# Reading position biases as one run of 157 numbers and spreading them on VectorE, in a hybrid attention and state-space kernel on Trainium2

## The chip, the cores and the metric

The kernel runs on one core of one Trainium2 chip. The metric is device time in microseconds of one execution; less is better. The time before is the median of three runs, 1765.67 us (1764.33 to 1768.28).

A core has five engines that each work through a queue of their own, in order: TensorE (matmuls, in the profile PE, its weight loads PEld), VectorE (DVE), ScalarE (ACT), GpSimd (POOL) and SyncE (SP, which in this kernel only issues DMAs). Data sits in SBUF, 128 partitions wide, and matmul results in PSUM, eight banks of 128 x 512 numbers here. Engines wait for each other through semaphores.

## The reference, cut to what matters

Two layers over 256 latent tokens of width 2048 and 256 context tokens. The first layer has 16 heads of 2-D neighbourhood attention beside a bidirectional state-space mixer; the second is a gated short convolution. The change touches the attention's position bias:

```python
GRID_W, NA_HEADS, NA_KH, NA_KW = 64, 16, 8, 16
rows = seq // GRID_W                       # 4 rows of 64 columns
kh = min(NA_KH, rows)                      # 4: every key row is seen
...
dc_idx = jnp.clip(col[None, :] - col[:, None], -(NA_KW - 1), NA_KW - 1) + NA_KW - 1
...
dr_idx = rs + jnp.arange(kh) - r + NA_KH - 1
bias = rpb[:, dr_idx[None, :, None], dc_idx[:, None, :]].reshape(nh, GRID_W, kh * GRID_W)
s_lat = jnp.einsum('bqhd,bkhd->bhqk', qr, kb).astype(jnp.float32) * scale + bias.astype(jnp.float32)
s_lat = jnp.where(mask, s_lat, -jnp.inf)
```

`rpb` has, for each head, 15 row differences x 31 column differences. A query at row r and column q needs, for key row a and key column b, the number at row difference a - r + 7 and column difference b - q + 15. Outside a window of 16 columns the score is masked, so what is added there does not matter as long as it is finite. Scores against the 256 context tokens have no bias. A softmax runs over 256 latent and 256 context keys.

## The kernel before, in words

**Weights.** All large matmuls take float32 inputs in two parts, a high part (a rounded copy, type fp32r) and a low part (the rest), and three products make one: high x high, high x low, low x high. Weights come from HBM in pieces of 128 x 1024 numbers (512 KB) into buffers called `raw` (`issue`, line 428, on SP's queue). ScalarE makes the high part `wH` (`split`, line 458), VectorE the low part `wL` (`low_part`, line 465), and the `raw` buffer is free again; TensorE multiplies (`mm`, line 231). There are three pairs of `wH` and `wL`. The same queue brings the pieces of the modulation matrix `in_ada_w`, which VectorE folds into a running sum (line 857).

**Order.** Nothing is scheduled at run time. While the program is built, a planner (`Plan`) keeps a clock for each engine and one for the DMA queue and prices every instruction. Side work is written as generators that yield what they wait for: `W_("DVE", bt)` goes on when the planner's clock of VectorE has room and `bt` is planned to be ready within 400 ns (`may`, lines 296 to 318). Between groups of matmuls, `pump` lets every such task go on as far as it can. A DMA on SP is priced in `Plan.add` with 450 ns of SP's time, and its bytes at 270 B per ns on the planner's DMA clock:

```python
            self.t[e] = s + (1200 if e == "POOL" else 450)
            if e == "SP":
                self.dma = max(self.dma, s + 1000) + n / self.RATE
```

A VectorE instruction with two full inputs is priced by the number of its elements. So the order of the instructions on each queue follows from these prices.

**Stages.** The modulated inputs are made (to about 200 us), then come the input projections, group by group (four heads of attention, two groups of the state-space mixer), with the attention heads and the state-space groups as side work between the matmuls; the last attention heads end near 1200 us. Then the output projection, the second layer's projections and its output follow.

**The bias.** Before the first head, one DMA (line 967) copies, for each head, 320 of the 15 x 31 numbers of `rpb`, from the 76th on, to an HBM scratch `rpbs` of [16, 64, 320], 64 times over: one copy for each query column. A bias buffer (two of them, `bias0` and `bias1`, taken in turn by the heads) is `bt`, 128 x 3 x 256: three blocks of 256 numbers in each partition. Block 0 is the bias of the first 128 queries (grid rows 0 and 1), block 1 of the other 128 (rows 2 and 3), each for 4 key rows x 64 key columns; partition p is grid row p // 64 of its half and query column p % 64. Block 2 is zero and stands for the context keys.

Each head (`head_gen`) first issues, on SP, four loads, one for each query row r, to 64 partitions of block r // 2 (line 1080). A partition gets four pieces of 64 numbers, 31 apart in the scratch, since neighbouring key rows are 31 numbers apart in `rpb`. The step of 319 between partitions in a scratch with rows of 320 slides the window by one number for each query column. VectorE then adds the mask in place, in one instruction over 2 x 4 x 64 numbers (line 1085). Later `top` (line 1098) adds the bias to the scores of a half, taking the row maximum at once. Loads of the head after the next must wait until this head's result is out (line 1077).

The steps that the prediction speaks of besides: `dt_gen` loads a row of biases and decay rates (`in_rows`, line 1184) to 128 partitions with SP's queue, and VectorE uses it at line 1203; this happens near the first two heads' bias loads. Shifted reads in the convolution of the second layer are at line 1856, a read of the same kind without a shift at line 1411.

Of the kernel before, what the change touches and what calls it, by code (L numbers as in the profile page):

```python
# [11 lines left out]
ALU = mybir.AluOpType  # L12
# [159 lines left out]
def kernel(ctx: ExitStack, tc, x, cx, ada_w, ada_b, w_in, w_out, sc_in, sc_out, rpb, small, const,  # L172
# [9 lines left out]
    V, S, G, T, DMA = nc.vector, nc.scalar, nc.gpsimd, nc.tensor, nc.sync  # L182
    DMA2 = nc.scalar
    plan = Plan()
    E = plan.add
# [214 lines left out]
    ident, strip, mask, mhalf = C_("ident"), C_("strip"), C_("mask"), C_("mhalf")  # L400
# [673 lines left out]
    def head_gen(a, h):  # L1074
        hd = 4 * a + h
        bt, s4 = bias[hd % 2], s4s[hd % 4]
        yield when(lambda: hd < 2 or ("pv", hd - 2) in got)
        yield W_("SP")
        for r in range(4):
            E(DMA.dma_start(bt[64 * (r % 2):64 * (r % 2) + 64, r // 2, :].rearrange("p (a b) -> p a b", a=4),  # L1080
                            bass.AP(tensor=b0.tensor, offset=b0.offset + hd * 64 * 320 + (7 - r) * 31 - 61,
                                    ap=[[319, 64], [31, 4], [1, 64]])))
        yield W_("DVE", bt)
        bv = bt[:, 0:2, :].rearrange("p q (r c) -> p (q r) c", c=64)
        E(V.tensor_tensor(out=bv, in0=bv, in1=mask.unsqueeze(1).to_broadcast([128, 8, 64]), op=ALU.add))
        sps = {}

        def score(qt):
# [461 lines left out]
    for h in range(4):  # L1550
        spawn(side, head_gen(0, h))
# [11 lines left out]
    def do_qk(a, nxt):  # L1563
        psQ = banks(2)
        proj(512, "act", psQ, 4)
        spawn(urgent, kq_gen("Q", a, psQ, 2, statq, QT, True), 2)
        psK = banks(4)
        proj(512, "act", psK, nxt)
        spawn(urgent, kq_gen("K", a, psK, 4, statk, KT, True), 4)
        for h in range(4):  # L1570
            spawn(side, head_gen(a, h))
# [432 lines left out]
```

## Time and profile before

The profiled execution took 1762.67 us; from its first to its last instruction it is 1760.9 us. The runs shown for comparison have their median 3.0 us above it.

| what | value |
|---|---|
| median of 3 runs | 1765.67 us |
| profiled execution | 1762.67 us, span 1760.9 us |
| mean granted TensorE clock | 0.999 |
| bias loads (line 1080) | 64 of 64 KB |
| mask adds (line 1085) | 16, mean 682 ns, 10.7 us together |
| DMA packets under 512 B | 34,304 of 147,629 |
| DMA engines' share by SP's queue | 64.0% |

How to read it. Busy time is time in which an engine executes; the profile also tells after which event an engine that stood idle went on ("releaser"). The chain that ended last is followed back from the last instruction, at each step to what released it. A DMA's issue is an instruction on the queue of its engine (SPq, POOLq); its data lands later. "x64" is a count; three durations with slashes are the least, the median and the greatest in ns. In the rows by stretch of time, each engine has its busy time and in brackets its instructions; then come TensorE's granted clock, the mean busy share of the 16 DMA engines (it can come out slightly over 1 in short stretches, since a packet counts where it begins) and what they moved in GB/s. In rows in order of time the first number is the start, the second the time until the last of the merged instructions ended, both in us; a bracket at the end is idle time of that engine before it and its releaser.

### The profile page before, as it was taken

What the parts mean: (1) busy time and instruction counts of PE and PEld (TensorE: products, weight loads), DVE (VectorE), ACT (ScalarE), POOL (GpSimd) and SP (SyncE); (2) the same over time, 40 slices, a digit from 0 to 9 for tenths busy, and PEclk for the clock granted to TensorE, in tenths of its full rate; (3) what the DMA queues carried; (4) which work ended last, traced back from release to release, by engine and by line L of the source; (5) the groups of instructions that cost most, each with busy time, mean ns of one, the idle gap of its engine ahead of it and who ended that gap; (6) DMA issues with size and microseconds to landing.
All of it is one profiled execution on the core that took longest, in us unless ns stands there. A gap on an engine that the chain in (4) does not pass through costs nothing.

```text
span 1760.9 us, 25272 instructions
## 1 busy us (share of the span) xinstructions
PE 1728.3 (98%) x9305; PEld 1442.4 (82%) x9305; DVE 1292.8 (73%) x2041; ACT 785.3 (45%) x1186; POOL 191.0 (11%) x300
## 2 busy tenths in 40 slices
PE   6999999999999999999999999999999999999998
PEld 4677988889888889888888898888878888888887
DVE  5566877888787987786888698876667776766555
ACT  5422335454354453353453444654435444444442
POOL 0000111013111012111012101110000000000000
PEclk9999999999999999999999999999999999999999
DMA  9987675577876677866577767787766888876774
GB/s 349 344 291 252 214 227 181 181 214 241 261 227 201 190 219 248 262 193 204 170 239 227 215 188 226 224 261 253 268 216 232 265 281 266 267 248 216 219 231 158
DMA packets 147629, 412.50 MB, mean 234 GB/s; under 512 B 34304, under 2 KB 48272, under 8 KB 147504
## 3 DMA queue, kind: packets, MB, share of 16 engines
q1 hardware_dynamic: 132112, 366.64, 64.0%
q0 software_dynamic: 15392, 44.24, 8.0%
q8 instruction: 73, 1.20, 0.3%
q14 instruction: 52, 0.43, 0.1%
HBM read 386.53 MB, written 25.59 MB: 234 GB/s over the span
## 4 chain that ended last, share of the span: by engine, by line
PE 94%; DVE 2%; DMA 1%; ACT 1%; issue 1%; SPq 0%; POOL 0%; DVEq 0%; ACTq 0%; POOLq 0%
PE bank L231 93%; PE bank L235 1%; DVE wL L465 1%; DMA raw<-in_ada_w 0%; ACT wH L458 0%; DMA half<-in_rows 0%; DVE hL L804 0%; SPq L618 0%; DMA raw<-in_sc_in 0%; DVE tmp L1283 0%; DVE h L1729 0%; DVE tmp L800 0%; ACT h L1748 0%; ACT hH L798 0%; DVE xm L664 0%
## 5 line engine op out<-in xcount | busy, mean ns | idle before, releaser
L458 ACT CAST wH<-raw 128x1024 fp32r<-128x1024 f32 (+1 forms) x440 | 459.5, 1045 | 664.0 <-PE bank L231 559.6
L465 DVE TENSOR_TENSOR wL<-raw,wH 128x1024 fp32r<-128x1024 f32 (+1 forms) x440 | 532.2, 1213 | 257.4 <-ACT wH L458 255.0
L231 PE MATMUL bank<-hH,wH 128*128 128x256 f32 (+1 forms) x1040 | 341.0, 328 | 0.9 <-ACT wH L458 0.9
L231 PE MATMUL bank<-hL,wH 128*128 128x256 f32 (+1 forms) x1040 | 337.0, 324 | 0.0
L231 PE MATMUL bank<-hH,wL 128*128 128x256 f32 (+1 forms) x1024 | 331.4, 324 | 3.1 <-DVE wL L465 3.1
L231 PE MATMUL bank<-wH,h 128*128 128x512 f32 x1024 | 316.8, 390 | 1.7 <-DVE h L1729 1.7
L231 PE MATMUL bank<-wH,hH 128*128 128x512 f32 x640 | 256.0, 400 | 4.8 <-ACT hH L798 2.6
L231 PE MATMUL bank<-wL,hH 128*128 128x512 f32 x640 | 249.9, 391 | 0.3 <-DVE wL L465 0.3
L231 PE MATMUL bank<-wH,hL 128*128 128x512 f32 x640 | 249.3, 390 | 0.1
L231 PEld LDWEIGHTS bank<-wH,h 128*128 128x128 f32 x1024 | 191.9, 188 | 43.5 <-DVE h L1729 3.0
L231 PEld LDWEIGHTS bank<-hH,wH 128*128 128x128 f32 x1040 | 197.8, 190 | 18.9 <-issue 2.0
L231 PEld LDWEIGHTS bank<-hL,wH 128*128 128x128 f32 x1040 | 197.8, 190 | 15.8
L231 PEld LDWEIGHTS bank<-hH,wL 128*128 128x128 f32 x1024 | 194.6, 190 | 19.4 <-DVE wL L465 4.1
L857 DVE SCALAR_TENSOR_TENSOR acc<-raw,csil,acc 128x512 f32<-128x512 f32 x240 | 179.1, 746 | 30.9 <-DMA raw<-in_ada_w 27.2
L231 PE MATMUL bank<-wL,h 128*128 128x512 f32 x512 | 199.4, 389 | 0.2 <-DVE wL L465 0.2
L231 PE MATMUL bank<-wH,mix 128*128 128x512 f32 x512 | 160.9, 391 | 0.0
L231 PEld LDWEIGHTS bank<-wH,hH 128*128 128x128 f32 x640 | 120.1, 188 | 36.3 <-issue 7.2
L231 PEld LDWEIGHTS bank<-wH,hL 128*128 128x128 f32 x640 | 120.1, 188 | 25.4 <-DVE hL L804 0.6
L231 PEld LDWEIGHTS bank<-wL,hH 128*128 128x128 f32 x640 | 120.1, 188 | 25.0 <-DVE wL L465 1.1
L231 PEld LDWEIGHTS bank<-wL,h 128*128 128x128 f32 x512 | 96.1, 188 | 20.6 <-DVE wL L465 0.6
L231 PEld LDWEIGHTS bank<-wH,mix 128*128 128x128 f32 x512 | 96.1, 188 | 20.4 <-issue 0.5
L231 PE MATMUL bank<-wL,mix 128*128 128x512 f32 x256 | 99.7, 390 | 0.0
(276 smaller groups left out, 1856.5 us busy)
## 6 DMA issues: line engine op xcount, KB each, us to landing
raw<-in_w_in SPq DMA_DIRECT2D x209, 512.0 KB
raw<-in_ada_w SPq DMA_DIRECT2D x163, 512.0 KB
raw<-in_sc_in SPq DMA_DIRECT2D x128, 512.0 KB
raw<-in_w_out SPq DMA_DIRECT2D x64, 512.0 KB
raw<-in_sc_out SPq DMA_DIRECT2D x32, 512.0 KB
dram_ptd<-tmp POOLq DMA_DIRECT2D x32, 256.0 KB, 4.9
D<-dram_ptd POOLq DMA_DIRECT2D x64, 128.0 KB, 5.6
tmp<-dram_csr SPq DMA_DIRECT2D x32, 256.0 KB
```

The lines of the kernel that those rows point to most:

```text
L231: E(T.matmul(o, l, r, start=start, stop=stop, skip_group_check=True))
L235: E(T.transpose(o, i, ident if k == 128 else ident[:k, :k]))
L458: E(S.copy(H, v))
L465: E(V.tensor_tensor(out=Lo, in0=v, in1=H.bitcast(F32), op=ALU.subtract))
L857: E(V.scalar_tensor_tensor(out=acc, in0=v[:, j], scalar=csil[:, 2 * k + j:2 * k + j + 1], in1=acc, op0=ALU.mult, op1=ALU.add))
```

## The change

The four loads of a head no longer bring four pieces of 64 numbers to each partition but one run of 157, which holds them all: 3 x 31 + 64 = 157. The run goes to the last 157 of the block's 256 places, from place 99 on. The add of the mask then reads its first input with an access pattern of its own, four runs of 64 that begin 31 apart and so overlap, and writes the 4 x 64 places of the block as before. Input and output share the buffer: for key row a and column b it reads place 99 + 31a + b and writes place 64a + b. The number of loads, their order, the waits and the instruction count are as they were in the text of the program; the planner's price of a load changes with its bytes.

```diff
         for r in range(4):
-            E(DMA.dma_start(bt[64 * (r % 2):64 * (r % 2) + 64, r // 2, :].rearrange("p (a b) -> p a b", a=4),
+            E(DMA.dma_start(bt[64 * (r % 2):64 * (r % 2) + 64, r // 2, 99:],
                             bass.AP(tensor=b0.tensor, offset=b0.offset + hd * 64 * 320 + (7 - r) * 31 - 61,
-                                    ap=[[319, 64], [31, 4], [1, 64]])))
+                                    ap=[[319, 64], [1, 157]])))
         yield W_("DVE", bt)
-        bv = bt[:, 0:2, :].rearrange("p q (r c) -> p (q r) c", c=64)
-        E(V.tensor_tensor(out=bv, in0=bv, in1=mask.unsqueeze(1).to_broadcast([128, 8, 64]), op=ALU.add))
+        run = bt[:, 0:2, 99:]
+        E(V.tensor_tensor(out=bt[:, 0:2, :].rearrange("p q (r c) -> p q r c", c=64),
+                          in0=bass.AP(tensor=run.tensor, offset=run.offset, ap=[list(run.ap[0]), [256, 2], [31, 4], [1, 64]]),
+                          in1=mask.unsqueeze(1).unsqueeze(1).to_broadcast([128, 2, 4, 64]), op=ALU.add))
```

## The prediction

> **What bounds the kernel now.** I read the engine shares, the chain that ended last, and then the bias tile. The page says:
>
> ```profile
> span 1760.9 us, 25272 instructions
> PE 1728.3 (98%) x9305; PEld 1442.4 (82%) x9305; DVE 1292.8 (73%) x2041; ACT 785.3 (45%) x1186; POOL 191.0 (11%) x300
> DMA packets 147629, 412.50 MB, mean 234 GB/s; under 512 B 34304, under 2 KB 48272, under 8 KB 147504
> PE 94%; DVE 2%; DMA 1%; ACT 1%; issue 1%; SPq 0%; POOL 0%; DVEq 0%; ACTq 0%; POOLq 0%
> ```
>
> TensorE is busy for 98% of the span and carries 94% of the chain. DMA packets and VectorE work count only where they make TensorE wait. So the first question is where the touched instructions lie (instructions of the bias tile), and how long TensorE stands still in that stretch (the busy times of the stretch, then TensorE's waits in it):
>
> ```profile
> L1080 SPq DMA_DIRECT2D bias<-dram_rpbs x64: 574/615/2323, 225.1 to 1137.8; - x64
> L1085 DVE TENSOR_TENSOR bias<-bias,const x16: 650/684/704, 234.7 to 1143.1; 128x512 f32<-128x512 f32 x16
>   DMA bias<-dram_rpbs: 0.8, 1
> 225.00:1160.00 935.00, 931.54 (x5257) 798.40 (x5256) 747.16 (x1281) 432.56 (x719) 139.91 (x212) 1.00 0.69 216
> PE bank L231 <- DVE wL L465: 2.8, 2, 2.3
> PE bank L231 <- ACT Vt L1050: 0.6, 1, 0.6
> ```
>
> The 64 loads and 16 adds lie between 225 and 1160 us. The add waited for its load once in 16, for 0.8 us. In these 935 us TensorE's busy time leaves 935.00 - 931.54 = 3.46 us of idleness, of which one stop is 2.3 us. Nothing that the change does to this stretch can gain more than those 3.46 us. I take 0.2% of the time, 3.5 us, as what a measurement of this kernel can tell from no change, so the whole idle time of the stretch is just at that bound.
>
> **Where that stop comes from.** The chain of waits from 234 us, then the first column of times on VectorE and TensorE, shows it whole:
>
> ```profile
> 234.79 0.33 SPq L428
> 235.17 7.13 DMA half<-in_rows
> 242.40 0.09 DVE half L1203
> 242.74 1.23 DVE wL L465
> ...
> 234.69 1.28 DVE L1085 TENSOR_TENSOR bias<-bias,const 128x512 f32<-128x512 f32 x2
> 242.40 0.43 DVE L1203 TENSOR_TENSOR half<-half,half 128x256 f32<-128x256 f32 x1 [6.09 <-DMA half<-in_rows]
> 242.74 2.35 DVE L465 TENSOR_TENSOR wL<-raw,wH 128x1024 fp32r<-128x1024 f32 x2
> ...
> 244.01 0.39 PE L231 MATMUL bank<-hH,wL 128*128 128x256 f32 x1 [2.33 <-DVE wL L465]
> ```
>
> A small load (the row of dt biases, issued at L1184) takes 7.13 us to land. VectorE, which works in order, stands 6.09 us in front of L1203; the two low parts of the weights (L465) are behind it, and TensorE waits 2.33 us for the first. What stands ahead of that load on SP's queue is the first two heads' bias loads and five weight loads (the queue in order of time):
>
> ```profile
> 225.08 7.26 SPq L1080 DMA_DIRECT2D bias<-dram_rpbs  x8
> 232.44 1.02 SPq L428 DMA_DIRECT2D raw<-in_w_in  x2
> 233.55 0.86 SPq L428 DMA_DIRECT2D raw<-in_ada_w  x2
> 234.79 0.33 SPq L428 DMA_DIRECT2D raw<-in_w_in  x1
> SPq L1080 <- DMA raw<-in_w_in: 2.1, 1, 2.1
> ```
>
> So this is the one place where the changed loads touch TensorE: eight of the 64.
>
> **Part 1: fewer and larger packets.** From the code, a bias load goes from 64 x 4 runs of 256 B (65,536 B) to 64 runs of 628 B (40,192 B). The kernel sheds 64 x 192 = 12,288 packets, and of its 34,304 under 512 B it loses 64 x 256 = 16,384. No view times one packet, so I bound their price by single microseconds (last two columns: share of the 16 DMA engines, GB/s) and the packets of 229 to 234 us:
>
> ```profile
> 231.00:232.00 1.00, 1.00 (x7) 0.81 (x6) 0.96 (x2) 0.00 (x0) 0.00 (x0) 1.00 1.36 205
> 232.00:233.00 1.00, 1.00 (x9) 0.96 (x8) 0.83 (x2) 0.54 (x1) 0.00 (x0) 1.00 0.42 66
> 233.00:234.00 1.00, 1.00 (x10) 1.00 (x10) 0.46 (x1) 0.99 (x2) 0.00 (x0) 1.00 0.47 94
> 237.00:238.00 1.00, 1.00 (x11) 1.00 (x10) 0.00 (x0) 0.79 (x1) 0.00 (x0) 1.00 1.03 422
> DMA packets 2287, 0.90 MB, mean 180 GB/s; under 512 B 2195, under 2 KB 2195, under 8 KB 2287
> ```
>
> Weights alone (237 to 238) move 422 / 1.03 = 410 GB/s per full share; with bias packets (231 to 232) it is 205 / 1.36 = 151 GB/s. Eight bias loads are 524,288 B: 1.3 us at 410, 3.5 us at 151. Afterwards they are 321,536 B: 0.8 us at 410, 2.1 us at 151. The saving lies between 1.3 - 0.8 = 0.5 us (small packets cost nothing extra) and 3.5 - 0.8 = 2.7 us. I take the middle, 1.6 us; it is near 3.5 - 2.1 = 1.4 us as well.
>
> There is also a hole. From 232 to 234 us the DMA engines are busy 0.42 and 0.47, so (1 - 0.42) + (1 - 0.47) = 1.1 us pass unused, because SP issues the first weight load at 232.44 only, after a bias load that had waited 2.1 us. The view names an earlier weight load as what ended that wait; in the code the bias tile depends on no weight, so it may be room in the queue, which 64 packets instead of 256 would ease. This is worth between 0 and 1.1 us; I take 0.3, the low side, as the cause is only guessed.
>
> A 628-B packet against the 256-B ones is not in the trace; if each cost as much as its bytes, the above holds, and if runs were cut in two there would still be 128 for 256.
>
> The sum: the small load lands 1.6 + 0.3 = 1.9 us earlier (bounds 0.5 and 3.8), and L1203, the low part behind it and TensorE with them. TensorE can gain no more than its 2.33 us there. What is next late: the high part that the second low part needs, and TensorE's own queue:
>
> ```profile
> 238.49 1.05 ACT L458 CAST wH<-raw 128x1024 fp32r<-128x1024 f32 x1 [0.22 <-PE bank L231]
> 241.41 0.28 PE L231 MATMUL bank<-hL,wH 128*128 128x256 f32 x1
> ```
>
> That cast ended at 239.5 and TensorE has work until 241.7, so neither is late within 1.9 us: with L1203 at 240.5 the first low part ends at about 242.1 and TensorE goes on then in place of 244.01. Thus **1.9 us**, between 0.5 and 2.33.
>
> [...] This case's drop from 410 to 151 GB/s with small packets speaks against bytes alone.
>
> **Part 2: the other 56 loads.** The same saving falls on heads 2 to 15. There TensorE's idleness is 3.46 - 2.33 = 1.13 us in all, and the add waited once, for 0.8 us. What hides them: the next head's scores wait for the turn of the heads, so a bias is loaded well ahead of its use, and TensorE has projections queued. Worth nothing. SP's issue time may fall (compare a weight load's, below), but SP's queue mostly waits for buffers:
>
> ```profile
> L428 SPq DMA_DIRECT2D raw<-in_sc_in x128: 327/328/332, 1295.7 to 1648.9; - x128
> SPq L428 <- DVE wL L465: 882.3, 373, 9.2
> ```
>
> **Part 3: the add.** It has as many elements as before and stays one instruction; only its first input is read as four overlapping runs of 64 that start 31 apart, two of them at an odd word. Nearest rows, two-source instructions in SBUF, straight and shifted by one word:
>
> ```profile
> L1411 DVE SCALAR_TENSOR_TENSOR yi<-tmp,small,tmp 128x256 f32<-128x256 f32 x16 | 7.7, 484 | 0.5
> L1856 DVE SCALAR_TENSOR_TENSOR v<-u,scwh,v 128x255 f32<-128x255 f32 x16 | 7.7, 478 | 0.0
> ```
>
> 484 ns straight and 478 shifted: a start at an odd word costs nothing, and neither row suggests a gain. I take 684 ns again. The upper bound is the step between those instructions and a second pass of 255 elements, 478 ns more for each add, 16 x 0.48 = 7.6 us over a stretch in which VectorE has 935 - 747 = 188 us free. At the one critical place two adds stand ahead of L1203, at 234.69; the 6.09 us of waiting after them swallow 2 x 0.48 = 0.96 us. Zero on the path. If the shorter load took that cover away, 4 us of it would still be there.
>
> [...]
>
> **Part 4: the order.** The program's order comes from a planner that charges a load its bytes at 270 B/ns and 450 ns of SP time. A bias load's charge falls from 243 to 149 ns, under the 450 of its issue, so its planned DMA clock moves by at most 0.38 us a head. Tasks are let in with a margin of 400 ns after groups of matmuls, so some adds, and some casts behind them, can come out a group earlier or later. TensorE does the same work. Zero, with the risk priced below.
>
> **The sum.** The profiled execution took 1762.67 us, 1.8 above its span and 3.0 below the median of the runs shown, 1765.67. Less 1.9 that is 1760.8 for such an execution, and 1763.8 for the median: 0.11%, too little to tell from no change.
>
> **Rivals.**
> - *Hidden anyway.* The small load's landing is set by the five weight loads alone: 5 x 524,288 B at 410 GB/s are 6.4 us of the 7.13. [...] For it: the DMA engines are idle at 0.42 just before. Against: that hole itself comes from SP being behind the bias loads.
> - *A worse order, slower.* A bias add, or another reader of a load, comes out one place earlier on VectorE, ahead of a low part, and waits there for its packets; TensorE starves. The price is in the trace: 6.09 us of such waiting became 2.33 us on TensorE. One event cancels the gain. It decides from the third event if the gain stays (3 x 2.33 - 1.9 = 5.1 us, 1770.8) or the second if it doesn't (4.7 us, 1770.3). For it: the margin of 400 ns is close to the shift of 0.38 us, and 16 heads try. Against: plan and chip both move the landing earlier, so the add should find its data.
> - *A better order.* The other 1.13 us go too: 1765.67 - 3.46 = 1762.2, and with luck among the stops after 1160 us a little less.
> - *It does not do what it says.* The add writes where it reads. It reads word 99 + 31a + b when it writes 64a + b, 99 - 33a >= 0 words ahead, so one rising pass reads each word before it is lost. I see no case here that costs time.
>
> **How the numbers follow.** Forecast (1.4 to 2.4 us gained) 0.45; hidden 0.30; worse order beyond the bound 0.12; better order beyond it 0.07; smaller shifts of order, 1761 to 1769, the rest. The range takes in the better order with a median as far off as the runs shown lie apart, 1764.33 to 1768.28, and the second event: 1760 to 1770. Faster 0.08 and slower 0.13 are the two cases beyond the bound with a hundredth each for what the small shifts may add; same is what is left, 0.79.
>
> **What would show it.** Right: packets near 135,300, with 17,920 under 512 B; the bias adds at 0.68 us; L1203's wait under 5 us and TensorE's stop near 242 us under 1 us; TensorE's idleness in 225 to 1160 us between 1 and 3 us. Wrong: the stop unchanged (hidden); adds over 0.75 us (reading); new rows of TensorE waiting for a low part, or VectorE waiting for bias (order).

## The result and the profile after

The changed kernel takes 1781.74 us (median of 6 runs, 1777.93 to 1786.39) beside 1766.63 us for the kernel before (6 runs): a ratio of 1.0079, 95% interval 1.0063 to 1.0094; the medians lie 15 us apart. Its profiled execution took 1781.08 us, its span is 1779.3, 18.4 us more than before. The page of the changed kernel, in the lines that answer to those shown of before:

```profile
span 1779.3 us, 25271 instructions
PE 1735.6 (98%) x9305; PEld 1446.5 (81%) x9305; DVE 1293.2 (73%) x2041; ACT 784.7 (44%) x1186; POOL 191.1 (11%) x300
DMA packets 135341, 410.88 MB, mean 231 GB/s; under 512 B 17920, under 2 KB 35984, under 8 KB 135216
PE 83%; DVE 7%; DMA 6%; issue 1%; ACT 1%; SPq 0%; POOL 0%; DVEq 0%; ACTq 0%; POOLq 0%
```

The packets are what the code says: 12,288 fewer, and 16,384 fewer under 512 B. VectorE does the same work. But the chain has lost 11 points from TensorE to VectorE and the DMAs, and TensorE both idles longer (1779.3 - 1735.6 = 43.7 us, before 1760.9 - 1728.3 = 32.6) and is busy longer (7.3 us more for the same 9305 matmuls): 11.1 + 7.3 = 18.4, the whole difference between these two executions. The execution of before is a quick one: its 1762.67 us lie below all 6 of the runs beside it (1764.33 to 1773.46). The instructions of the bias tile, the busy times of the stretch from 225 to 1160 us, and TensorE's waits up to 1180 us, all of the changed kernel:

```profile
L1080 SPq DMA_DIRECT2D bias<-dram_rpbs x64: 445/594/1652, 226.0 to 1156.1; - x64
L1085 DVE TENSOR_TENSOR bias<-bias,const x16: 649/685/702, 234.0 to 1161.5; 128x512 f32<-128x512 f32 x16
...
225.00:1160.00 935.00, 920.70 (x5179) 787.33 (x5178) 733.53 (x1252) 419.97 (x698) 137.31 (x209) 0.99 0.67 210
...
PE bank L231 <- DVE wL L465: 4.7, 3, 2.5
PE bank L231 <- DVE half L1492: 3.4, 1, 3.4
PE bank L231 <- ACT qH L1121: 2.8, 1, 2.8
PE bank L231 <- DVE tmp L1469: 1.0, 1, 1.0
```

The loads' issue and the add cost what they did (594 against 615 ns, 685 against 684). Yet TensorE's idleness in the stretch went from 3.46 to 935.00 - 920.70 = 14.30 us. The two largest new stops wait for VectorE's line 1492 (a sum of squares of the state-space mixer) and for a part of an attention query (line 1121; lines after the add are two higher than before). Neither is touched by the change.

**What stands behind these stops.** The chain of waits of the changed kernel, from 395 us:

```profile
395.32 9.19 DMA raw<-in_ada_w
404.51 0.02 issue
404.54 0.75 DVE acc L857
405.29 0.60 DVE tmp L1100
...
406.00 0.43 DVE half L1492
406.43 0.04 issue
406.47 5.91 PE bank L231 x15
```

VectorE's queue in order of time at that place and at the next, with TensorE's two stops below:

```profile
404.54 0.75 DVE L857 SCALAR_TENSOR_TENSOR acc<-raw,csil,acc 128x512 f32<-128x512 f32 x1 [4.80 <-DMA raw<-in_ada_w]
405.20 0.68 DVE L1100 CUSTOM_DVE_ANT_1 tmp<-bank,bias 128x512 f32<-128x512 f32 x1
406.00 0.42 DVE L1492 TENSOR_TENSOR half<-half,half 128x256 f32<-128x256 f32 x1
...
478.73 1.54 DVE L857 SCALAR_TENSOR_TENSOR acc<-raw,csil,acc 128x512 f32<-128x512 f32 x2 [4.69 <-DMA raw<-in_ada_w]
480.19 1.30 DVE L250 STREAM_TRANSPOSE KT<-kqD_K 128x512 f32<-128x512 f32 x2
...
406.47 1.01 PE L231 MATMUL bank<-const,half 128*128 128x1 f32 x4 [3.43 <-DVE half L1492]
482.60 0.50 PE L231 MATMUL bank<-kH,qH 128*128 128x512 f32 x1 [2.75 <-ACT qH L1121]
```

Twice VectorE stands for almost 5 us in front of a step of the running sum (line 857), whose piece of `in_ada_w` has not landed: at 404.5 us the load has been under way for 9.19 us. What is queued behind that step in VectorE's order is what TensorE needs next: the sum of squares at 406, the turned keys at 480. Over the whole span VectorE waits for these pieces 27.2 us in the kernel before (first row) and 47.6 in the changed one:

```profile
DVE acc L857 <- DMA raw<-in_ada_w: 27.2, 14, 3.8
DVE acc L857 <- DMA raw<-in_ada_w: 47.6, 22, 5.6
```

TensorE's longer busy time has its place there as well. The stretches around the first stop and, last, after the second place (the third number from the end is the granted clock):

```profile
402.00:406.00 4.00, 1.05 (x5) 0.52 (x3) 1.43 (x4) 0.00 (x0) 0.00 (x0) 0.99 0.46 150
406.00:410.00 4.00, 3.53 (x10) 3.00 (x11) 3.80 (x13) 3.76 (x8) 0.66 (x1) 0.50 0.01 2
410.00:414.00 4.00, 4.00 (x13) 3.12 (x12) 2.55 (x7) 1.63 (x5) 1.33 (x3) 0.66 0.93 265
414.00:418.00 4.00, 4.00 (x35) 3.93 (x33) 3.51 (x7) 3.73 (x6) 0.54 (x1) 1.00 0.52 177
484.00:488.00 4.00, 4.00 (x18) 2.70 (x17) 1.27 (x5) 1.39 (x4) 0.60 (x1) 0.57 0.31 118
```

After the stop of 3.43 us TensorE has 0.50 and 0.66 of its clock for eight microseconds, of which it works 3.53 and 4.00 us, so the stop costs about 3.53 x 0.50 + 4.00 x 0.34 = 3.1 us once more. After the second place (2.75 us and, half a microsecond on, 0.54) it is at 0.57 from 484 to 488 us: 4 x 0.43 = 1.7 us. The two make 4.8 of the 7.3 us by which TensorE is busy longer. The stop of 2.33 us in the kernel before was followed by a clock of 1.00.

**The order.** The queues of the two programs differ. On VectorE's queue the first difference is the one that the prediction named, the first add one place earlier:

```diff
 L857 SCALAR_TENSOR_TENSOR acc<-raw_138,csil,acc 128x512 x2
-L465 TENSOR_TENSOR wL_145<-raw_137,wH_142 128x1024
 L1085 TENSOR_TENSOR bias_217<-bias_217,const 128x512
+L465 TENSOR_TENSOR wL_145<-raw_137,wH_142 128x1024
 L1085 TENSOR_TENSOR bias_218<-bias_218,const 128x512
```

That one dies out. The next difference comes at 390 us of the kernel before, and from there the orders differ on all five queues. Compared in the two traces by line, operation and tile (buffer numbers left out), the queues differ up to 783 us and are the same again from there to the end. The time is lost where they part: the TensorE matmul in the same place of its queue comes 0.3 us later in the changed kernel at 265 us, 15.0 at 476 us, 17.4 at 766 us and 18.4 at the end. TensorE's busy time from 265 to 500 us, before and then changed (the first number after the stretch is its length, the next TensorE's busy time):

```profile
265.00:500.00 235.00, 235.00 (x1305) 200.40 (x1304) 186.06 (x330) 108.28 (x181) 41.85 (x65) 1.00 0.71 217
265.00:500.00 235.00, 225.80 (x1240) 191.45 (x1239) 177.69 (x320) 104.46 (x178) 40.16 (x61) 0.98 0.65 201
```

### The profile page after: what moved, and what is told of

Same layout as the page of the kernel before. It is cut to its first block, busy times and chain, and to the rows that moved or that the text cites. A ratio compares the mean times of both kernels' runs of the same rounds, so it can differ in the third digit from the quotient of the medians.

```text
span 1779.3 us, 25271 instructions
## 1 busy us (share of the span) xinstructions
PE 1735.6 (98%) x9305; PEld 1446.5 (81%) x9305; DVE 1293.2 (73%) x2041; ACT 784.7 (44%) x1186; POOL 191.1 (11%) x300
## 4 chain that ended last, share of the span: by engine, by line
PE 83%; DVE 7%; DMA 6%; issue 1%; ACT 1%; SPq 0%; POOL 0%; DVEq 0%; ACTq 0%; POOLq 0%
PE bank L231 82%; DMA raw<-in_ada_w 4%; DVE wL L465 2%; PE bank L235 1%; DVE acc L857 1%; DVE tmp L1285 1%; DMA tmp<-dram_csr 1%; ACT wH L458 0%; DMA raw<-in_w_in 0%; DMA half<-in_rows 0%; DMA bias<-dram_rpbs 0%; DMA xs<-in_x 0%; DVE D L1147 0%; DVE hL L804 0%; DMA raw<-in_sc_in 0%
## 5 line engine op out<-in xcount | busy, mean ns | idle before, releaser
L857 DVE SCALAR_TENSOR_TENSOR acc<-raw,csil,acc 128x512 f32<-128x512 f32 x240 | 179.3, 747 | 51.3 <-DMA raw<-in_ada_w 47.6
```

Of the source, the lines that this page charges most:

```text
L857: E(V.scalar_tensor_tensor(out=acc, in0=v[:, j], scalar=csil[:, 2 * k + j:2 * k + j + 1], in1=acc, op0=ALU.mult, op1=ALU.add))
```

## The experiments

Two theories. **O**: the new loads and the new add cost nothing on the chip; the planner charges a load fewer bytes, takes it to land up to 0.38 us earlier, and lets tasks out in another order, which is worse. **H**: the long loads or the overlapping read cost time themselves, in a way that the busy times don't show.

The two can be pulled apart, because the planner's charge is one number in its code. With the old charge the changed kernel has the order of the kernel before on all queues, and with the new charge the kernel before has that of the changed one; the traces agree, by line, operation and tile.

**e1: new loads, old charge.**

```diff
-            self.t[e] = s + (1200 if e == "POOL" else 450)
+            n, self.t[e] = (65536 if outs[0].tensor.name.startswith("bias") else n), s + (1200 if e == "POOL" else 450)
```

> The changed kernel, with the planner made to charge a bias load its old 65,536 B, so that every queue has the order of the kernel before. Theory O (the 15 us come from the planner's other order): within 3 us of the kernel before, 1763 to 1768, if anything about 2 us faster by the shorter stop near 242 us. Theory H (the 157-number loads or the overlapping read cost time on the chip itself): as slow as the changed kernel, 1777 to 1786.

**e2: old loads, new charge**: the same edit with 40192, in the kernel before.

> The kernel before with its four runs of 64 and its add in place, but the planner charges a bias load 40,192 B, which gives every queue the order of the changed kernel. Theory O: 1777 to 1787, as slow as the changed kernel or a little slower, with TensorE's stops of about 3.4 us near 400 to 440 us and 480 us. Theory H: 1763 to 1769.

**e3: new loads, new charge for the first eight alone**, 65,536 for the other 56.

> The changed kernel; the planner charges 40,192 B for the first eight bias loads and 65,536 B for the other 56. The order is that of the kernel before but for the first bias add, which comes ahead of a low part (L465) on VectorE instead of behind it. Theory O with the later loads to blame: 1762 to 1768. If the slip of that first add is what costs: several us above e1. Theory H: 1777 to 1786.

**e4: new loads, a charge of 50,000 B.**

> The changed kernel with the planner charging 50,000 B for a bias load, a third order that shares little with either. If any other order is worse than the one before (theory O in its strong form): 1775 to 1790. If orders scatter and the changed kernel drew a bad one: anywhere from 1764 to 1785. Theory H: 1777 to 1786, like every kernel with the new loads.

Measured against the kernel before, beside them on the same chip (1769.36 us): e1 1769.3 us, 0.9996 (0.9981 to 1.0012); e2 1782.44 us, 1.0084 (1.0059 to 1.0110); e3 1768.21 us, 0.9990 (0.9979 to 1.0001); e4 1784.11 us, 1.0081 (1.0061 to 1.0101). H has fallen: the new loads without the new order cost nothing that can be measured, and the new order without the new loads costs all of it. Its two stops stand there too, 4.06 us at 407.65 and 3.18 us at 483.93, with the same chain in front of the first:

```profile
396.85 8.84 DMA raw<-in_ada_w
...
405.71 0.75 DVE acc L857
...
407.18 0.42 DVE half L1490
```

e3 shows that the slip of the first add is harmless. e4 shows that a third order, with the same loads, is as bad as the second. The stop that the prediction was about did not go in e1, though. TensorE's rows of e1 at its stops over 1.5 us:

```profile
245.98 0.38 PE L231 MATMUL bank<-hH,wL 128*128 128x256 f32 x1 [2.47 <-DVE wL L465]
398.77 0.65 PE L231 MATMUL bank<-tmp,xtm 128*64 128x128 f32 x6 [1.54 <-DVE tmp L1469]
```

**e5 and e6: no waiting for in_ada_w.** What in the order costs? e5 has the order of the changed kernel and e6 that of the kernel before (e1's), both with the new loads. The steps of the running sum read a constant tile; the planner still counts them as reading the piece, so that no queue changes its order.

```diff
-                        E(V.tensor_scalar(out=acc, in0=v[:, j], scalar1=csil[:, 0:1], scalar2=None, op0=ALU.mult))
+                        setattr(plan, 'sub', v[:, j]); E(V.tensor_scalar(out=acc, in0=strip[:, :512], scalar1=csil[:, 0:1], scalar2=None, op0=ALU.mult))
...
-                    E(V.scalar_tensor_tensor(out=acc, in0=v[:, j], scalar=csil[:, 2 * k + j:2 * k + j + 1], in1=acc,
+                    setattr(plan, 'sub', v[:, j]); E(V.scalar_tensor_tensor(out=acc, in0=strip[:, :512], scalar=csil[:, 2 * k + j:2 * k + j + 1], in1=acc,
```

> The changed kernel with its own order on every queue, but the running sum of the modulation (L855 and L857) reads a constant tile in place of the pieces of in_ada_w, so VectorE no longer waits for those loads; they are still loaded. This leaves the second layer's modulation out. If VectorE's waits for in_ada_w, at places where the planner took them to have landed, make TensorE's extra stops: the stops near 406 and 482 us go, no drop of the granted clock after them, 1763 to 1771. If the order costs through something else (matmuls too early on TensorE's queue, casts, weight loads): 1776 to 1782.

> The same removal in the changed kernel with the old order (e1). If waits for in_ada_w are what separates the orders, they cost little here: 1761 to 1768, within 3 us of e5. If removing them gains as much here as in e5, the two orders stay 10 us or more apart and the waits are not what separates them.

e5: 1765.51 us, 0.9984 (0.9973 to 0.9994) of the kernel before (1768.87 us beside them); e6: 1766.18 us, 0.9983 (0.9973 to 0.9993). The order that cost 0.79% costs nothing any more when VectorE doesn't wait for those pieces, and the two orders take the same time. In e5 the stop near 406 is gone, and where the changed kernel had 2.75 and 0.54 us there is left:

```profile
473.21 0.50 PE L231 MATMUL bank<-kH,qH 128*128 128x512 f32 x1 [0.87 <-ACT qH L1121]
474.25 0.50 PE L231 MATMUL bank<-kH,qL 128*128 128x512 f32 x1 [0.54 <-DVE qL L1124]
```

The edit frees the pieces' buffers earlier too, so it takes away the waits and whatever follows from them together; that the waits themselves start it is read from the chains above.

**e7 and e8: a later step.** The planner lets a step out when its load has landed by its own clock plus 1 us. If that is too hopeful, more should help: 3 us in e7, 5 us in e8, in the complete changed kernel.

```diff
-        late = eng[-1] == "+"
+        late = len(eng) - len(eng.rstrip("+"))
...
-        rdy = plan.ready(aps) + (1000 if late else 0)
+        rdy = plan.ready(aps) + 1000 * late
...
-                yield W_("DVE+", RAW["gem", n, k][1])
+                yield W_("DVE+++", RAW["gem", n, k][1])
```

> The changed kernel, complete, with the planner told to let a running-sum step out only 3 us (in place of 1 us) after it takes its load to have landed: another order again. If the waits for in_ada_w are the cause: their sum on VectorE falls below the 26 us of the kernel before and the time comes to 1760 to 1772. If orders are merely drawn at random: anywhere from 1764 to 1786.

> The same with 5 us. If the waits are the cause: as good as the 3 us or better, 1759 to 1770, unless the running sum then falls behind its use at the second layer, which would show as stops after 1290 us. If orders are drawn at random: anywhere from 1764 to 1786.

Both are far slower: 1820.12 us, 1.0290 (1.0269 to 1.0311), and 1840.35 us, 1.0405 (1.0382 to 1.0427). e7 missed, in the time and in the waits (36.3 us, not under 26); e8 came out by the exception that its expectation names. The sum comes too late for the second layer. TensorE's waits of e8 from 1150 to 1400 us:

```profile
PE bank L231 <- DVE acc L857: 57.7, 2, 40.2
PE bank L235 <- DMA rowb<-dram_mrow: 6.5, 1, 6.5
```

Before that e8 is the best of all: from 225 to 1160 us VectorE doesn't wait for a piece at all (its 45.2 us of such waits come later), and TensorE is idle for 1.52 us only. This takes the waits out of that stretch without freeing a buffer early, and points the same way as e5. e7 has 8.5 us of these waits left there and yet two stops of over 4 us; in front of the one of 4.42 us at 470.07 VectorE stands before another load, that of the turned keys:

```profile
467.65 1.30 DVE L250 STREAM_TRANSPOSE KT<-kqD_K 128x512 f32<-128x512 f32 x2 [5.15 <-DMA kqD_K<-dram_kqd]
```

So the steps can stand in the way or come late, and a margin trades one for the other.

**e9: the row of dt biases ahead.** This tests the prediction's first part by itself: e3 with the small load issued before the first heads' loads, into a tile that is not yet in use.

```diff
-    csr, exr = drt([64, 256], "csr"), drt([64, 256], "exr")
+    csr, exr, rowt, row_load = drt([64, 256], "csr"), drt([64, 256], "exr"), wst.rearrange("p a b -> p (a b)"), []; row_load.append(DMA.dma_start(rowt, rows[0].partition_broadcast(128)))
...
-        E(DMA.dma_start(rw[:, :128], rows[0].partition_broadcast(128)))
+        E(row_load[0])
```

> e3 (new loads, the order of the kernel before but for the first add) with the load of the row of dt biases issued ahead of the bias and weight loads, into a tile that is free then; nothing else changes its place on any queue. If that load's landing behind five weight loads makes the stop near 242 us: L1205 no longer waits, the stop of 1.4 to 2.5 us goes, 1 to 2.5 us faster than e3, 1762 to 1767. If something else stops TensorE there (a cast, a weight load): the stop stays, the time is that of e3.

1766.03 us beside 1770.1 for the kernel before, 0.9978 (0.9968 to 0.9987): faster, beyond the interval, and the fastest complete kernel here. Against e3 (0.9990) the intervals overlap, so a gain in time from this step alone isn't shown; that the stop goes is, in the trace. VectorE's rows of e9, where the kernel before had waited 6.09 us at this step:

```profile
235.29 0.42 DVE L1203 TENSOR_TENSOR half<-bank,half 128x256 f32<-128x256 f32 x1
235.75 0.43 DVE L1205 TENSOR_TENSOR half<-half,wst 128x256 f32<-128x256 f32 x1
237.00 1.23 DVE L465 TENSOR_TENSOR wL<-raw,wH 128x1024 fp32r<-128x1024 f32 x1 [0.83 <-ACT wH L458]
```

TensorE has no stop near 242 us any more.

**e10 to e12: three more orders** of the complete changed kernel: 5 us of margin for the first four of 16 column groups, 2 us for all, and a charge of 75,000 B.

> The changed kernel, complete; the planner lets running-sum steps out 5 us after their load for the first four of the 16 column groups and 1 us after it for the rest, so that the sum can catch up before the second layer. If late waits for in_ada_w and a sum that is late at its use were the two costs of e7 and e8, both shrink: 1760 to 1775. If orders are drawn at random: 1764 to 1786.

> The changed kernel with a margin of 2 us for all running-sum steps. Between the changed kernel (1 us) and e7 (3 us, sum late at its use): 1765 to 1800; if the lateness at the second layer begins only at 3 us, 1762 to 1775.

> The changed kernel with the planner charging 75,000 B for a bias load, more than before: a further order. If a dearer price keeps running-sum steps behind their loads: 1762 to 1772. If a change of 0.1 to 0.4 us in a planned landing just draws another order: 1764 to 1786, with VectorE's waits for in_ada_w and the stops of 3 us and more deciding where.

1772.6 us, 1.0020 (1.0008 to 1.0032); 1772.96 us, 1.0018 (1.0006 to 1.0030); 1774.22 us, 1.0032 (1.0016 to 1.0047), beside the same 1770.1 us. All between the two orders. e11 has the shortest waits for the pieces, 9.4 us, and still stops 3.2 us near 1028 us for a low part and 3.6 us near the second layer, so these waits are what made the changed kernel's order bad, but not the only thing that can.

All kernels side by side; the three right-hand columns are from one profiled execution each (idle: TensorE, 225 to 1160 us; waits: VectorE's at lines 855 and 857 for pieces of in_ada_w, whole span). Executions of one order differ: e1, with the order and the time of the kernel before, idled 5 us more than that kernel's quick execution, so such a step in a column says little by itself:

| kernel | order | ratio | idle, us | longest stop there, us | waits, us |
|---|---|---|---|---|---|
| before | before's | 1 | 3.46 | 2.33 | 27.2 |
| changed | its own | 1.0079 | 14.30 | 3.43 | 47.6 |
| e1 | before's | 0.9996 | 8.70 | 2.47 | 34.9 |
| e2 | the changed one's | 1.0084 | 15.69 | 4.58 | 43.5 |
| e3 | before's but one add | 0.9990 | 5.31 | 1.39 | 33.8 |
| e4 | third | 1.0081 | 13.76 | 3.09 | 59.1 |
| e5 | the changed one's, no waits | 0.9984 | 3.85 | 1.83 | 0 |
| e6 | before's, no waits | 0.9983 | 5.51 | 2.88 | 0 |
| e7 | its own | 1.0290 | 11.11 | 4.42 | 36.3 |
| e8 | its own | 1.0405 | 1.52 | 0.96 | 45.2 |
| e9 | e3's, row ahead | 0.9978 | 3.10 | 1.14 | 32.0 |
| e10 | fourth | 1.0020 | 4.43 | 1.60 | 28.4 |
| e11 | fifth | 1.0018 | 4.50 | 3.23 | 9.4 |
| e12 | sixth | 1.0032 | 9.12 | 2.25 | 32.7 |

The sum of the waits doesn't rank the kernels (e1 and e12 have about the same); what counts is what stands behind a wait in VectorE's queue.

## Why the prediction was wrong

**What held.** TensorE bounds the kernel (98% of the span busy, before and after), and only what makes it wait counts. The 56 later loads are worth nothing that e1 could measure (0.9996), the packets came out to the number, and the add keeps its duration in spite of two runs that start at an odd word and of rows that overlap. Its group in the changed kernel, by line and shape (682 ns before as well):

```profile
L1085 DVE TENSOR_TENSOR bias<-bias,const 128x512 f32<-128x512 f32 x16 | 10.8, 682 | 1.2 <-DMA bias<-dram_rpbs 1.2
```

**The step that failed: part 4, "Zero, with the risk priced below."** The order was given no cost, and a worse one beyond the bound a chance of 0.12. It was the whole result: 1.0084 with the old loads (e2), 0.9996 with the new loads in the old order (e1). The mechanism of that rival was the right one: a reader of a load comes out too early on VectorE and TensorE starves behind it. Three things in it were off. First, the reader was not a bias add but the running sum, which reads 128 loads of 512 KB against the 64 small ones. The prediction did name "another reader of a load", but weighed the risk at the instructions of the change, when a planner hands a small shift on to the tasks that follow, here over some 390 us. Against it stood that plan and chip both move the landing earlier; that holds for the bias alone. Second, its price, 2.33 us for an event, left out the clock: the stops of 3.43 us and of 2.75 with 0.54 us in the changed kernel took 3.1 and 1.7 us more through it. Third, the 3.46 us for which the kernel before idles in 935 bound what can be gained; they don't bound what can be lost, as the orders of e2, e4 and the changed kernel (13.8 to 15.7 us of idleness) show.

**Part 1 was wrong as well, and would have been a miss of up to 2 us.** The forecast had the small load land 1.9 us earlier through lighter packets, and TensorE's stop near 242 us come under 1 us. In the order of before with the new loads the stop is 2.47 us (e1) and 2.88 (e6), not shorter than 2.33. With the first add ahead it is 1.70 us in the changed kernel and 1.39, 1.83 and 1.79 in e3, e5 and e4, against 4.58 in the one execution of that order with the old loads (e2): there the new loads may shorten it, but nowhere by as much as forecast, and the times of e1 and e3 show no gain. No run measures the larger term, 1.6 us for the packets, by itself. SP's queue in e1 shows what kept the loads back:

```profile
226.54 8.38 SPq L1080 DMA_DIRECT2D bias<-dram_rpbs  x8
235.02 1.02 SPq L428 DMA_DIRECT2D raw<-in_w_in  x2
236.12 0.86 SPq L428 DMA_DIRECT2D raw<-in_ada_w  x2
237.08 0.55 SPq L428 DMA_DIRECT2D raw<-in_w_in  x1
237.68 0.44 SPq L1186 DMA_DIRECT2D half<-in_rows  x1
```

Beside it stands what SP waited for there, and, in another view, the DMA engines' share (second number from the end), both of e1:

```profile
SPq L1080 <- DMA raw<-in_w_in: 3.6, 2, 3.0
```

```profile
232.00:234.00 2.00, 2.00 (x12) 1.68 (x11) 1.84 (x2) 0.91 (x3) 0.00 (x0) 1.00 0.76 158
234.00:236.00 2.00, 2.00 (x17) 1.79 (x15) 1.91 (x4) 1.44 (x2) 0.00 (x0) 1.00 0.15 40
```

The eight issues still took 8.38 us (7.26 before), with 3.6 us of waiting for an earlier weight load's landing where there had been 2.1; a quarter of the packets did not ease it. The hole in which the DMA engines have little to do is still there, at a share of 0.15 from 234 to 236 us, and the five weight loads and the small one come no sooner after the first bias load. The rival "hidden anyway" was right there in its outcome; its reason, the five weight loads, is a part of it only, since SP reaches them late for its own wait. e9, which moves the small load out from behind them, has the stop gone that the forecast wanted to shorten.

**What is left open.** How often an order drawn by another charge or margin is good: besides that of the kernel before (with e3's and e9's, which differ from it by one add and one small load) seven orders ran with the whole work, those of the changed kernel, e4, e7, e8, e10, e11 and e12, and none beat it. Why a piece took 9.19 us from issue to landing near 395 us, against a median of 4.8 in the stretch, was not taken apart; from 394 to 402 us the DMA engines were busy at 0.92 to 1.05. The DMA wait of SP's issues was seen, not explained. And the chain from a late piece to TensorE is shown for the large stops of the changed kernel, e2 and e4; e7 and e11 have large stops that start elsewhere.

## What to carry to other kernels

Where a program's order is made by a planner that prices its instructions, a change of a price can be a change of every queue for hundreds of microseconds: first make the edit with the old price, so that the order stays, and measure that; then look for the order by itself. Read a small idle time of the bound engine as the most to gain, and not as the most to lose. And before a load's packets are made better, see whether the next loads wait for packets or for the queue that issues them.

## What the runs showed of the hardware that was not expected

**TensorE's clock after a stop.** In the profiled executions of all fourteen kernels TensorE stops 28 times for 1.5 us or more between 225 and 1325 us. Each of the twelve stops of 2.75 us and more was followed by a lowered granted clock (0.50 to 0.73 in a stretch of four microseconds after the stops of 3.43 and 2.75 us in the changed kernel, 4.06 and 3.18 in e2, 3.09 in e4, 4.42 and 4.20 in e7 and 3.23 in e11). Of the sixteen from 1.54 to 2.48 us nine were (1.60 to 2.21 us) and seven were not (among them 2.33 us in the kernel before and 2.48 in the changed one, each with a clock of 1.00 in the four microseconds after it). At the same place, after 1.70 us (changed kernel, first row) and 1.83 us (e5), the next four microseconds read:

```profile
244.31:248.31 4.00, 4.00 (x28) 3.78 (x29) 3.97 (x6) 1.15 (x3) 0.09 (x1) 1.00 0.60 189
244.65:248.65 4.00, 4.00 (x21) 4.00 (x22) 3.97 (x6) 0.15 (x1) 0.09 (x1) 0.57 0.61 189
```

Busy time times the missing share of the clock, over the eight microseconds after a stop, gives an estimate of what it costs besides itself: 1.7 us for each of the nine (e5: 4.00 x 0.43), and 1.5 to 3.4 us for the long ones (e8's left out, since TensorE soon stops again there), the most after 3.09 us in e4 and 3.43 us in the changed kernel (3.4 and 3.1 us). What decides whether a stop of about 2 us lowers the clock no run here shows.

**A queue that waits with little in it.** SP's eight bias issues waited 2.1 us (before) and 3.6 us (e1) for the landing of an earlier weight load that the bias tile does not depend on, with 256 packets each and with 64. The wait does not go with the packets: it is 3.1 us in e2 with 256, and 2.1 to 3.9 us in the changed kernel, e3 to e7, e9 and e12 with 64, where the eight issues take 6.86 to 8.56 us; in the orders of e8, e10 and e11 they take 5.00 to 5.26 us and wait 0.5 us at most.
